# A tuned hybrid decoder block: two mixer forms rounded behind copies of products, three up weights' low parts behind the second token tile, gated tiles and a down sum ahead of low parts

## The chip, the cores and the metric

The kernel runs on one core of one Trainium2 chip. Its time is the device time of one execution, in microseconds (us). Three executions of the kernel before took 708.55, 709.43 and 709.46 us; the median is 709.43. A further execution was recorded by the hardware profiler; all rows of the profile and all durations are from that one.

## The reference, cut to what matters

One decoder layer on 512 tokens of 1024 channels, everything in float32:

```
h = rms_norm(x);  z = h @ w_in
y_pool = pool_mixer(z[pool]) @ w_pool_out
y_rnn  = rg_lru(z[rx]) * gelu(z[rg]) @ w_rg_out
x = x + rms_norm((sigmoid(z[gate_pool]) * y_pool + sigmoid(z[gate_rnn]) * y_rnn) @ w_o)
h = rms_norm(x);  up = h @ w_up                      # 1024 -> 2 x 3072
x = x + rms_norm((gelu(causal_conv(up[:3072])) * up[3072:]) @ w_down)
x = x + sigmoid(rms_norm(x) @ w_ple_gate) * rms_norm(p @ w_ple_proj)
```

## The kernel before

Engines are called by their short names: PE multiplies matrices, ACT (scalar engine) and DVE (vector engine) do the elementwise work, POOL (GpSimd) issues some transfers and takes the powers in the norms, SP issues the other transfers.

**Products.** A float32 product is made of three matmuls: every operand is split into a high part, which is the operand rounded to the type fp32r by a cast on ACT, and a low part, which the DVE makes by subtracting the high part from the operand. The helper `split` (L195 for the cast, L191 for the subtraction) and `prep` (L449, L191) do this; `mm3` (L222 to L224) issues high by high, high by low and low by high. Each split therefore costs one cast on ACT and one subtraction on DVE, and every matmul waits for them. The large products are moreover made in seven instead of eight block products (forms 1 to 7, in the order of `SEVEN`, `RSEVEN` and `SERIAL`). For these, sums and differences of blocks of the activations ("forms") are made on DVE and split, and sums of blocks of the weights lie in DRAM, made by transfers that POOL issues. Results of seven products are put together by copies and sums out of the PSUM banks (`ps`).

**Stages**, in the order of the PE: the input product with the mixers; the merge of the two mixers, which works on the products `rg` with w_rg_out (`rg_product`, two halves p, each with the forms 1, 5, 6, 2, 3, 7, 4); the w_o product in seven forms (`product("wo", ...)` with `o_form`); the first norm, per token tile of 128 tokens (four tiles); the product for the per-layer embedding (`ple_tile`, 12 matmuls of 512 columns for each tile); twelve pairs of tiles of the up product, the first one in plain blocks 11, 21, 12, 22 (`up_plain`, weights by `up_form(0, f)`), the others in seven forms (`up_product`); gating (`gated_half`, `hidden`); the down product in seven forms (`down_form`); and the per-layer gate. A token tile t goes through `x2_sum` and `x2_out`: two squares on ACT (L483), a sum s on DVE (L494), a power on POOL (L478), two `scalar_tensor_tensor` (L980) that make the residual, the same chain again for the next norm, and two more (L1053) that write the normalised halves `h2n`. `h2_tile` transposes each half on the PE (L991), splits it (cast L195 on ACT, low part L191 on DVE, both into tiles named `C`) and copies quarters of it to `h2f` on ACT (L1017).

**What sets the order.** The PE's order is the order of the code. The other engines' order is made ahead of time by a scheduler, which takes priorities: `urgent()` and `high_priority` put an instruction ahead of those recorded before it. Within an engine instructions run strictly in that order, so an instruction that waits holds up all behind it. `behind(ins, name)` adds an edge that orders `ins` after another instruction of the same engine. It adds no semaphore and no work.

**The names the change touches.** `last_copy` and `last_sub` hold the ACT cast and the DVE subtraction that `split` made last. `o_form(f)` (L878 to L891) makes form f of the merged activations for the w_o product and splits it into a quad `A`. Forms 1 and 2 are made within the second half of the merge, behind the products 6 and 7, the later ones within the w_o product. In `rg_product` a finished product f = 7 is copied twice by ACT, plain (L946) and negated (L947), to banks that the next products add onto. In the w_o product, L1067 copies the two banks of form 1 to the banks of form 2, and L1077 sums form 6 with form 5's copy into the banks of form 3. `up_form` makes the high and low part of a weight. In the gated stage, `hidden` (L1145) multiplies gate and up tiles into `h`; L1119 later writes negated products into the up banks that `hidden` reads. In the down product, L1350 subtracts product 7 from a kept copy `q5`, `down_form` makes and splits the forms, and L975 (`norm_of`) starts the next norm.

Edges that are in the kernel before and matter here: `up_form(1, f)` for f other than 1 has its cast behind `h2_done`, and for p above 2 form 6 has its cast behind `z_done`.

## Time and profile before

| what | value |
|---|---|
| three runs | 708.55, 709.43, 709.46 us, median 709.43 |
| the profiled execution | 708.84 us |
| its span | 707.1 us (1.74 us lie around it) |
| PE busy | 696.1 us, 98% of the span, 4423 instructions |
| PE weight loads (PEld) | 639.3 us, 90% (beside the matmuls) |
| DVE busy | 592.0 us, 84%, 772 instructions |
| ACT busy | 456.0 us, 64%, 693 instructions |
| POOL busy | 95.1 us, 13%, 123 instructions |
| mean granted clock of the PE | 0.996 |

How to read the views: a row of a timeline gives the start (us from the span's start), the duration, the engine, the line of the code, the operation, the tile written and the tiles read (buffer numbers left out), the size, how many instructions of this kind the row stands for, and, in brackets, the idle time ahead of the first of them and what ended it. A row of the view of waits gives who waited for whom, the total in us, how often and the longest. The view by windows gives busy microseconds of PE, PEld, DVE, ACT and POOL with their numbers of instructions, the granted clock of the PE, the share of the DMA engines, and GB/s. The busy time of the PE is near the whole span, so its few waits, and the stretches with a lower clock, are what is left beside the work itself.

### The profile page before, as it was taken

Reading aid. Unit: us, or ns where it says so; the run is one execution under the profiler, and the core shown is the slowest. Engines: PE = TensorE matmul, PEld = TensorE weight load, DVE = VectorE, ACT = ScalarE, POOL = GpSimd, SP = SyncE. Lnnn points to the kernel's source line nnn. Section 1 sums busy time; section 2 is a strip of 40 time slices with the busy share of each in tenths; the row PEclk is TensorE's granted clock in tenths of the full one; section 3 lists DMA queues with packets and bytes.
Section 4 is the critical chain, followed back from the end, with each engine's and each line's share of the span. In section 5 each row is a group of like instructions: output and inputs, shape, how many; then the busy total and the mean of one; then the engine's idle time right before and its main releaser. Section 6 shows DMA issues by size and latency. Waiting matters only on the chain.

```text
span 707.1 us, 11612 instructions
## 1 busy us (share of the span) xinstructions
PE 696.1 (98%) x4423; PEld 639.3 (90%) x4423; DVE 592.0 (84%) x772; ACT 456.0 (64%) x693; POOL 95.1 (13%) x123
## 2 busy tenths in 40 slices
PE   9999999999999999989999999999999999999997
PEld 7888888888889998879999999999999888888886
DVE  5698645999849898786989999999999998788972
ACT  5857789834547565478956776666667766665631
POOL 0321231421000000111013222221200000001100
PEclk9999999999999999999999999999999999999999
DMA  8999899999797897764379999999967576867111
GB/s 307 410 311 281 238 245 251 252 298 263 241 339 279 307 345 286 279 238 149 125 255 266 261 322 251 321 236 331 229 189 235 196 263 221 274 213 258 55 61 61
DMA packets 67288, 175.72 MB, mean 249 GB/s; under 512 B 6048, under 2 KB 6688, under 8 KB 66848
## 3 DMA queue, kind: packets, MB, share of 16 engines
q1 hardware_dynamic: 49808, 124.64, 49.9%
q0 software_dynamic: 17280, 50.34, 29.7%
q8 instruction: 35, 0.57, 0.3%
q14 instruction: 21, 0.17, 0.1%
q10 hardware_dynamic: 144, 0.00, 0.0%
HBM read 162.37 MB, written 62.91 MB: 319 GB/s over the span
## 4 chain that ended last, share of the span: by engine, by line
PE 84%; DVE 8%; ACT 3%; issue 2%; DMA 1%; POOL 1%; SPq 0%; ACTq 0%; DVEq 0%
PE ps L222 27%; PE ps L224 26%; PE ps L223 26%; PE ps L557 3%; DVE lo L191 2%; ACT rb L483 1%; PE ps L666 1%; DMA m<-in_x_t_dram 1%; DVE A L191 1%; POOL s L478 1%; DMA m<-in_rows_dram 1%; DVE m L1180 1%; DVE t L975 1%; DVE m L927 1%; ACT hi L195 1%
## 5 line engine op out<-in xcount | busy, mean ns | idle before, releaser
L191 DVE TENSOR_TENSOR lo<-raw,hi 128x1024 fp32r<-128x1024 f32 (+2 forms) x199 | 230.4, 1183 | 44.2 <-ACT hi L449 29.1
L222 PE MATMUL ps<-A,hi 128*128 128x256 f32 (+1 forms) x672 | 212.2, 316 | 0.8 <-ACT ps L1119 0.8
L223 PE MATMUL ps<-A,hi 128*128 128x256 f32 (+1 forms) x672 | 211.4, 315 | 0.0
L224 PE MATMUL ps<-A,lo 128*128 128x256 f32 (+1 forms) x672 | 211.4, 315 | 0.0
L449 ACT CAST hi<-raw 128x1024 fp32r<-128x1024 f32 (+1 forms) x118 | 118.3, 1013 | 57.0 <-PE ps L224 30.1
L222 PEld LDWEIGHTS ps<-A,hi 128*128 128x128 f32 x672 | 128.2, 191 | 9.3 <-issue 1.0
L224 PEld LDWEIGHTS ps<-A,lo 128*128 128x128 f32 x672 | 128.3, 191 | 6.9
L223 PEld LDWEIGHTS ps<-A,hi 128*128 128x128 f32 x672 | 128.2, 191 | 6.7
L222 PE MATMUL ps<-C,hi 128*128 128x256 f32 x376 | 103.7, 276 | 1.1 <-ACT ps L946 1.1
L224 PE MATMUL ps<-C,lo 128*128 128x256 f32 x376 | 103.2, 274 | 0.0
L223 PE MATMUL ps<-C,hi 128*128 128x256 f32 x376 | 103.2, 274 | 0.0
L195 ACT CAST hi<-raw 128x1024 fp32r<-128x1024 f32 x78 | 80.6, 1052 | 28.1 <-PE ps L223 18.3
L222 PE MATMUL ps<-hi,A 128*128 128x512 f32 x224 | 85.3, 381 | 0.6 <-ACT ps L1067 0.3
L223 PE MATMUL ps<-lo,A 128*128 128x512 f32 x224 | 84.9, 379 | 0.0
L224 PE MATMUL ps<-hi,A 128*128 128x512 f32 x224 | 84.9, 379 | 0.0
L222 PEld LDWEIGHTS ps<-C,hi 128*128 128x128 f32 x376 | 71.8, 191 | 1.8 <-ACT ps L946 1.3
L223 PEld LDWEIGHTS ps<-C,hi 128*128 128x128 f32 x376 | 71.8, 191 | 0.1
L224 PEld LDWEIGHTS ps<-C,lo 128*128 128x128 f32 x376 | 71.8, 191 | 0.0
L478 POOL TENSOR_TENSOR s<-s,mhalf 128x1 f32<-128x1 f32 (+1 forms) x21 | 15.2, 725 | 329.1 <-DVE s L494 306.4
L222 PEld LDWEIGHTS ps<-hi,A 128*128 128x128 f32 x224 | 42.3, 189 | 7.2 <-ACT ps L1067 0.7
L307 POOL DMA_DIRECT2D wdsum<-in_w_down_dram x36 | 33.3, 1087 | 110.2 <-ACT ps L1114 53.4
L224 PEld LDWEIGHTS ps<-hi,A 128*128 128x128 f32 x224 | 42.3, 189 | 6.0
(202 smaller groups left out, 1071.1 us busy)
## 6 DMA issues: line engine op xcount, KB each, us to landing
raw<-in_w_up_dram SPq DMA_DIRECT2D x46, 512.0 KB, 7.1
wdsum<-in_w_down_dram POOLq DMA_DIRECT2D x36, 512.0 KB, 9.7
raw<-in_w_in_dram SPq DMA_DIRECT2D x32, 512.0 KB, 7.8
raw<-wdsum SPq DMA_DIRECT2D x24, 512.0 KB, 4.3
raw<-in_w_down_dram SPq DMA_DIRECT2D x18, 512.0 KB, 4.2
wosum<-in_w_o_dram POOLq DMA_DIRECT2D x12, 512.0 KB, 8.7
wdsum<-wdsum POOLq DMA_DIRECT2D x12, 512.0 KB, 6.8
raw<-wosum SPq DMA_DIRECT2D x8, 512.0 KB, 6.7
```

Source lines behind the costliest of these rows:

```text
L191: return V.tensor_tensor(o, a, b, ALU.subtract)
L195: last_copy[0] = ACT.copy(hi, src)
L222: PE.matmul(o, ah, bh, start=start, stop=False, **kw)
L223: PE.matmul(o, ah, bl, start=False, stop=False, **kw)
L224: PE.matmul(o, al, bh, start=False, stop=stop, **kw)
L307: ins = nc.gpsimd.dma_start(o, i, **kw)
L449: ins = ACT.copy(hi, raw)
L478: last_pow[0] = nc.gpsimd.tensor_tensor(y, v, mhalf[:, :n], ALU.pow).ins.name
L483: ins = ACT.activation(rb, v, AF.Square, scale=1.0 / 32.0, accum_out=s)
L557: PE.matmul(rx[m], a[:, o : o + P], turns(b), start=k == 0 and i == 0, stop=k == KD - 1 and i == 2)
L666: PE.matmul(ps, bd[pr, a, o], turns(b[pr]), start=i == 0, stop=i == 2)
L927: V.tensor_tensor(g4, v.rearrange("p (h b a) -> p h a b", a=2, b=P), g4, ALU.mult)
```

## The change

All four parts add edges with `behind`; no instruction is added or removed on any engine.

1. In `o_form`, for the forms 2 and 5, the ACT cast is placed behind the instruction in `z_copied`: for form 2 the last negated copy of product f = 7 (L947), for form 5 the last copy L1067.
2. In `up_form(0, f)`, for f = 21, 12 and 22 the low part on DVE is placed behind the second half of `h2n` of token tile 1 (L1053), and for f = 12 and 22 the cast on ACT is placed behind the last ACT copy to `h2f` (L1017) that is recorded by then, of token tile 0.
3. In `up_form(1, 4)` the low part is placed behind the last gated tile `h` (L1145) that is recorded by then.
4. In `down_form(4, 2)` the low part is placed behind the first of the two sums L1350.

```diff
@@ -410,8 +410,14 @@
             t = b[p, {2: 21, 3: 22, 5: 0}[f]]
         hi, lo = (v.rearrange("p (j c) -> p j c", j=2) for v in parts_of(D))
         split(hi, lo, t)
+        if p == 0 and PLAIN.index(f) > 1:
+            behind(last_copy[0], h2f_done[0])
+        if p == 0 and PLAIN.index(f) > 0:
+            behind(last_sub[0], h2n_done[1])
         if p == 1 and f != 1:
             behind(last_copy[0], h2_done[0])
+        if (p, f) == (1, 4):
+            behind(last_sub[0], hid_done[0])
         if p > 2 and f == 6:
             behind(last_copy[0], z_done[0])
         ready["up", p, f] = (hi, lo)
@@ -812,6 +818,7 @@
 
 
     rp = {}
+    h2n_done, h2f_done, z_copied, hid_done, summed = {}, [None], [None], [None], {}
 
     def ple_tile(t):
         pair = []
@@ -887,6 +894,8 @@
             V.tensor_tensor(v, h11, h21, ALU.subtract)
         of[f] = quad("A").rearrange("p (s a) (b c) -> p s (a b) c", s=2, b=2)
         split(of[f][:, 0], of[f][:, 1], v)
+        if f in (2, 5):
+            behind(last_copy[0], z_copied[0])
 
     def o_lhs(f, k, i):
         v = of[f][:, :, k, i * P : (i + 1) * P]
@@ -944,7 +953,7 @@
                     ACT.activation(rb2[i][:, :HALF], z, AF.Identity, scale=-1.0)
                 elif f == 7:
                     ACT.copy(ra[i][:, HALF:], z)
-                    ACT.activation(rb2[i][:, HALF:], z, AF.Identity, scale=-1.0)
+                    z_copied[0] = ACT.activation(rb2[i][:, HALF:], z, AF.Identity, scale=-1.0).ins.name
             if p and f in (2, 3):
                 merge(p, int(f == 3), i, slice(0, HALF))
             elif f in (7, 4):
@@ -1014,7 +1023,8 @@
             if c == 0:
                 h2f[q] = {k: slot() for k in (0, 2)}
             for k in (0, 2):
-                ACT.copy(kept(h2f[q][k].rearrange("p (k c) -> p k c", k=2)[:, :, c * P : (c + 1) * P]), apart(ps[:, k : k + 2, :]))
+                v = kept(h2f[q][k].rearrange("p (k c) -> p k c", k=2)[:, :, c * P : (c + 1) * P])
+                h2f_done[0] = ACT.copy(v, apart(ps[:, k : k + 2, :])).ins.name
 
 
 
@@ -1050,7 +1060,8 @@
             r = rstd_of(res, after=after)
             for h in range(2):
                 h2n[t, h] = slot()
-                V.scalar_tensor_tensor(h2n[t, h], res[h], r, g_pre[h], ALU.mult, ALU.mult)
+                ins = V.scalar_tensor_tensor(h2n[t, h], res[h], r, g_pre[h], ALU.mult, ALU.mult)
+                h2n_done[t] = ins.ins.name
 
 
     o11, o12 = ra, rb2
@@ -1064,7 +1075,7 @@
                 o_form(SERIAL[n + 1])
             if f == 1:
                 with urgent():
-                    ACT.copy(o11[q - 2], oz[q - 2])
+                    z_copied[0] = ACT.copy(o11[q - 2], oz[q - 2]).ins.name
             if f == 7 and q == 2:
                 x2_norm(1, (o11[1], o12[1]))
             if last and q == 2:
@@ -1142,7 +1153,7 @@
                 ALU.add,
             )
             pu = hid[j]
-        V.tensor_tensor(hid[j], act_g[j], pu, ALU.mult)
+        hid_done[0] = V.tensor_tensor(hid[j], act_g[j], pu, ALU.mult).ins.name
 
     for t in range(NT):
         with tc.high_priority(offset=3 * URGENT):
@@ -1259,6 +1270,8 @@
             V.tensor_tensor(v, h11, h21, ALU.subtract)
         w = quad("A").rearrange("p (s a) (b c) -> p s (a b) c", s=2, b=2)
         split(w[:, 0], w[:, 1], v)
+        if (f, m) == (4, 2):
+            behind(last_sub[0], summed[0])
         down[f, m] = w
 
     def ahead_form(f, m):
@@ -1347,7 +1360,7 @@
         pass
     for i in range(2):
         with urgent():
-            V.tensor_tensor(q5[:, i], q5[:, i], zd[i], ALU.subtract)
+            summed[i] = V.tensor_tensor(q5[:, i], q5[:, i], zd[i], ALU.subtract).ins.name
     load_x3(1)
     x3_norm(0, (c11[0], c12[0]))
     x3_add(0)
```

In the changed kernel's file the lines stand 6 to 13 further down than in the one before (L946 is 955 there, L1067 is 1078, L1053 is 1063, L1017 is 1027, L975 is 984, L980 is 989, L826 is 833, L494 is 500, L1145 is 1156; L191 and L195 are the same).

What this does to the order on ACT at the merge and the first w_o product. `A` are the high parts of the forms (A441 is form 2, A472 form 5), `C427` the merged activations, `hi` the high parts of weights. Before:

```order
L946 COPY ps369_2057<-ps382_2131 128x256
L947 ACTIVATE ps377_2097<-ps382_2131 128x256
L195 CAST A441_2594<-C427_2479 128x1024
L946 COPY ps373_2077<-ps383_2132 128x256
L947 ACTIVATE ps381_2117<-ps383_2132 128x256
L449 CAST hi463_2663<-raw462_2661 128x1024
L449 CAST hi466_2688<-raw465_2686 128x1024
L1067 COPY ps369_2057<-ps457_2656 128x512
L449 CAST hi469_2701<-raw468_2699 128x1024
L195 CAST A472_2719<-C471_2717 128x1024
L1067 COPY ps373_2077<-ps458_2657 128x512
```

After:

```order
L955 COPY ps369_2057<-ps382_2131 128x256
L956 ACTIVATE ps377_2097<-ps382_2131 128x256
L955 COPY ps373_2077<-ps383_2132 128x256
L956 ACTIVATE ps381_2117<-ps383_2132 128x256
L195 CAST A441_2594<-C427_2479 128x1024
L455 CAST hi463_2663<-raw462_2661 128x1024
L455 CAST hi466_2688<-raw465_2686 128x1024
L1078 COPY ps369_2057<-ps457_2656 128x512
L455 CAST hi469_2701<-raw468_2699 128x1024
L1078 COPY ps373_2077<-ps458_2657 128x512
L195 CAST A472_2719<-C471_2717 128x1024
```

The two copies of the second product now stand ahead of form 2's cast, and the second L1067 copy ahead of form 5's.

On DVE at the second token tile, `lo538`, `lo554` and `lo558` are the low parts of the up weights 21, 12 and 22, m522 and m523 the normalised halves of token tile 1, s520 the sum of their norm, m453 and m454 the residual of token tile 2, m560 and m564 copies of embedding products, and C505 a low half of token tile 1. Before:

```order
L191 TENSOR_TENSOR lo538_3003<-raw536_3000,hi537_3002 128x1024
L191 TENSOR_TENSOR lo554_3036<-raw552_3033,hi553_3035 128x1024
L191 TENSOR_TENSOR lo558_3049<-raw556_3046,hi557_3048 128x1024
L494 SCALAR_TENSOR_TENSOR s520_2926<-s518_2922,s519_2924 128x1
L1053 SCALAR_TENSOR_TENSOR m522_2930<-m451_2644,s521_2928,m447_2635 128x512
L1053 SCALAR_TENSOR_TENSOR m523_2932<-m452_2646,s521_2928,m448_2636 128x512
L975 TENSOR_TENSOR t539_3012<-ps457_2656,m445_2631 128x512
L494 SCALAR_TENSOR_TENSOR s543_3020<-s541_3014,s542_3017 128x1
L826 COPY m560_3059<-ps555_3039 128x512
L826 COPY m564_3079<-ps562_3065 128x512
L980 SCALAR_TENSOR_TENSOR m453_2648<-t539_3012,s544_3022,m453_2648 128x512
L191 TENSOR_TENSOR C505_2882<-ps566_3085,C504_2881 128x4x128
```

After, from the first normalised half on (the sum s520 stands right ahead of it):

```order
L1063 SCALAR_TENSOR_TENSOR m522_2930<-m451_2644,s521_2928,m447_2635 128x512
L1063 SCALAR_TENSOR_TENSOR m523_2932<-m452_2646,s521_2928,m448_2636 128x512
L984 TENSOR_TENSOR t539_3012<-ps457_2656,m445_2631 128x512
L500 SCALAR_TENSOR_TENSOR s543_3020<-s541_3014,s542_3017 128x1
L833 COPY m560_3059<-ps555_3039 128x512
L989 SCALAR_TENSOR_TENSOR m453_2648<-t539_3012,s544_3022,m453_2648 128x512
L989 SCALAR_TENSOR_TENSOR m454_2650<-t540_3013,s544_3022,m454_2650 128x512
L984 TENSOR_TENSOR t575_3118<-sum461_2660,m446_2632 128x512
L833 COPY m564_3079<-ps562_3065 128x512
L191 TENSOR_TENSOR lo538_3003<-raw536_3000,hi537_3002 128x1024
L191 TENSOR_TENSOR lo554_3036<-raw552_3033,hi553_3035 128x1024
L191 TENSOR_TENSOR lo558_3049<-raw556_3046,hi557_3048 128x1024
```

The three low parts moved not only behind the two normalised halves but behind seven more instructions; the low half C505 of token tile 1 follows them now, as it did before. On ACT the casts of the weights 12 and 22 moved behind the four copies L1017 of token tile 0, and the squares of token tile 1's norm (L483) moved ahead of them. On SP three loads of sums of up weights (`raw<-up1sum`), which take the buffers of these three weights, are issued later, behind writes of results to DRAM.

On DVE at the first gated tiles, lo651 is the low part of up form (1, 4), lo654 and lo657 those of later weights, h647 and h648 the gated tiles. Before:

```order
L191 TENSOR_TENSOR lo651_3570<-raw649_3567,hi650_3569 128x1024
L1145 TENSOR_TENSOR h647_3563<-t637_3515,ps621_3303 128x512
L1145 TENSOR_TENSOR h648_3565<-t638_3521,ps622_3316 128x512
L191 TENSOR_TENSOR lo654_3602<-raw652_3599,hi653_3601 128x1024
L191 TENSOR_TENSOR lo657_3632<-raw655_3629,hi656_3631 128x1024
```

After:

```order
L1156 TENSOR_TENSOR h647_3563<-t637_3515,ps621_3303 128x512
L1156 TENSOR_TENSOR h648_3565<-t638_3521,ps622_3316 128x512
L191 TENSOR_TENSOR lo651_3570<-raw649_3567,hi650_3569 128x1024
L191 TENSOR_TENSOR lo654_3602<-raw652_3599,hi653_3601 128x1024
L191 TENSOR_TENSOR lo657_3632<-raw655_3629,hi656_3631 128x1024
```

The two gated tiles moved ahead of one low part; on ACT the two L1119 copies, which follow them, moved ahead of the fourth of four casts of weights. In the down product, the low part of form (4, 2) had stood ahead of the first sum L1350 and of a product `t` (L975); now `t` and the sum stand ahead of it, and the second `t` follows.

## The prediction

> **What bounds the kernel now.** I read the waits of the PE first, then the timelines of PE, ACT and DVE at each place where an edit falls, then the clock by windows. The view of waits lists, for each group, who was waited for, the us in total, how often, and the longest.
>
> ```profile
> PE ps L991 <- DVE m L1053: 1.6, 1, 1.6
> PE ps L222 <- ACT ps L946: 1.1, 1, 1.1
> PE ps L241 <- DVE mhalf L235: 1.1, 1, 1.1
> PE ps L222 <- ACT ps L1119: 0.8, 1, 0.8
> PE ps L991 <- DVE s L494: 0.5, 1, 0.5
> PE ps L557 <- ACT A L527: 0.5, 1, 0.5
> PE ps L222 <- ACT ps L1067: 0.3, 1, 0.3
> PE ps L222 <- DVE sum L1350: 0.3, 1, 0.3
> ```
>
> The PE is the bound, and it stands still only at single places of about a microsecond. The edits aim at six of these eight rows: L946 and L1067 (first edit), L1053 and L494 (second), L1119 (third), L1350 (fourth). Their sum, 4.6, is the most that the list itself promises. Two corrections follow. One is how a wait is counted: the list counts from the shown end of a matmul, but matmuls overlap.
>
> ```profile
> 258.90 0.28 PE L224 MATMUL ps<-A,lo 128*128 128x256 f32 x1
> 259.01 0.28 PE L222 MATMUL ps<-C,hi 128*128 128x256 f32 x1
> ```
>
> A 256-column matmul is shown 0.28 long, and the next starts 0.11 after it. A wait therefore costs about 0.17 more than listed. The other correction is larger: what is late next, once a wait is gone.
>
> **Place 1, merge and first w_o product (258 to 285).** ACT in before:
>
> ```profile
> 260.21 1.05 ACT L195 CAST A<-C 128x1024 fp32r<-128x1024 f32 x1 [1.70 <-DVE C L928]
> 261.17 0.37 ACT L946 COPY ps<-ps 128x256 f32<-128x256 f32 x1
> ```
> ```profile
> 268.42 1.05 ACT L195 CAST A<-C 128x1024 fp32r<-128x1024 f32 x1 [0.20 <-DVE C L878]
> 269.37 0.58 ACT L1067 COPY ps<-ps 128x512 f32<-128x512 f32 x1
> ```
>
> ACT stood idle 1.70 for the DVE's C, then rounded the form for 1.05, and only then copied a product that the PE had finished at 258.90 + 0.28 = 259.18. With the copy ahead it runs in that idle time. The listed 1.1 + 0.17 = 1.27 vanishes. So does the wait on the L1067 copy, which stood behind the cast of 268.42: 0.3 + 0.17 = 0.47. The PE is 1.74 earlier from 270 on. The first rounded form comes hardly later, since the copies fit into the 1.70 of idle time. The second now stands behind the L1067 copy of 0.58, about 0.5 later; queued behind it on ACT are only casts of weights. The next w_o products read the two forms, one of them 5 us away; I put the 0.5 at nothing, and at 0.5 without that cover. Next late is a sum on the DVE:
>
> ```profile
> 281.63 1.23 DVE L191 TENSOR_TENSOR A<-C,A 128x1024 fp32r<-128x1024 f32 x1 [0.21 <-ACT A L195]
> 282.77 0.69 DVE L1077 TENSOR_TENSOR ps<-sum,ps 128x512 f32<-128x512 f32 x1
> ```
> ```profile
> 284.35 0.38 PE L222 MATMUL ps<-hi,A 128*128 128x512 f32 x1
> ```
>
> L1077 ends at 283.46, and the PE adds onto its result at 284.35, 0.89 later. It stands behind a low part that waits for a cast of ACT, in a row of forms that no edit moves. The PE would come at 284.35 - 1.74 = 282.61, and find it ready only 283.46 plus some 0.06. So 0.91 of the 1.74 is given back: **-0.83**. Its ends are 0, if the row of forms slips as much again, and -1.74, if it moves with the PE. I take the middle, because the rows give it.
>
> **Place 2, second token tile (302 to 323).** DVE and ACT of before, and then three places of the PE:
>
> ```profile
> 302.63 3.49 DVE L191 TENSOR_TENSOR lo<-raw,hi 128x1024 fp32r<-128x1024 f32 x3
> 306.04 0.15 DVE L494 SCALAR_TENSOR_TENSOR s<-s,s 128x1 f32<-128x1 f32 x1
> 306.85 1.41 DVE L1053 SCALAR_TENSOR_TENSOR m<-m,s,m 128x512 f32<-128x512 f32 x2 [0.66 <-POOL s L478]
> 308.18 0.68 DVE L975 TENSOR_TENSOR t<-ps,m 128x512 f32<-128x512 f32 x1
> ```
> ```profile
> 301.89 1.05 ACT L195 CAST hi<-raw 128x1024 fp32r<-128x1024 f32 x1
> 302.84 0.64 ACT L483 ACTIVATE rb<-m 128x512 f32<-128x512 f32 x1
> ```
> ```profile
> 305.52 0.38 PE L223 MATMUL ps<-lo,m 128*128 128x512 f32 x1
> 305.73 0.38 PE L224 MATMUL ps<-hi,m 128*128 128x512 f32 x1
> 307.74 0.63 PE L991 MATMUL ps<-ident,m 128*128 128x128 f32 x4 [1.63 <-DVE m L1053]
> ```
> ```profile
> 316.27 0.27 PE L222 MATMUL ps<-C,hi 128*128 128x256 f32 x1
> ```
> ```profile
> 322.64 0.38 PE L222 MATMUL ps<-C,hi 128*128 128x256 f32 x1
> ```
>
> Three low parts of 3.49 stand ahead of the norm's sum s (L494). Behind them after the change, the sum waits only for its square, which takes the place of the cast at 301.89: about 301.9 + 0.64 + 0.1, so s at 302.7. With the same 0.81 from s to the halves (306.04 to 306.85), the halves are made from 303.5 to 304.9. The PE is free at 305.73 + 0.215 = 305.95 and finds them there: both stalls, 1.63 and 0.5, are gone. Eight transposes (0.63 for four, so about 1.0 for both halves) and the 24 matmuls before 316.27, at 0.215 each (305.52 to 305.73), put the first up matmul at about 312.0 instead of 316.27. This looks like 4.3, but the DVE pays. After the halves, from 304.9, come t and a copy (0.6 each), two L980 (1.3, released by POOL about then), another t and another copy: 3.8 in all. Only then, 308.7 to 312.1, come the three low parts; the low half of the second token tile, which the second up matmul reads, ends another 0.7 later, 312.8. The PE waits 0.8 there. Then a chain that the PE does not set:
>
> ```profile
> 318.21 1.41 DVE L980 SCALAR_TENSOR_TENSOR m<-t,s,m 128x512 f32<-128x512 f32 x2 [0.65 <-POOL s L478]
> ```
> ```profile
> 322.02 0.56 ACT L827 COPY m<-ps 128x512 f32<-128x512 f32 x1
> ```
>
> From the sum of the fourth tile, 0.8 ahead of 318.21, through L980 and four squares, to L827's copy, which ends at 322.58, 0.06 ahead of the matmul at 322.64 that takes its bank. This chain is why 322.64 was 322.64. After the change the low half at 312.8 releases ACT's copies of it (two sets of 0.6), a square of 0.64 on each side, and the sum comes at 316.1 rather than 317.4. Moving with it, the copy ends at 321.25. The PE's work from 316.27 to 322.64 holds 6.37, of which I take 6.2 to lie behind the second up matmul; it stands at its bank by 312.8 + 6.2 = 319.0, waits 2.3, and goes on at 321.30: **-1.34**. The ends: 0 where the chain is as late as before, and -4.3 where it follows the PE entirely. I take the chain's value since its durations are in the rows, and only its order differs. The three delayed low parts are read from about 315 on, when the first up product is through. The casts that the edit puts behind ACT's copies come before these low parts, and hold up only the next casts. SP's issues follow the buffers that these low parts free:
>
> ```profile
> 303.92 2.54 SPq L379 DMA_DIRECT2D raw<-up1sum  x3
> ```
>
> These three loads go out some 6 us later (low parts from 308.7 instead of 302.6), behind writes of results. They serve the second pair of up products, whose casts stand 30 us and more behind; I put them at nothing, and at up to 6 if they were wanted at once.
>
> The clock belongs to this place. Windows of before (the columns are busy us of PE, PEld, DVE, ACT, POOL, then the granted clock, DMA share and GB/s):
>
> ```profile
> 308.00:312.00 4.00, 3.45 (x14) 2.74 (x13) 4.00 (x9) 2.30 (x6) 0.54 (x1) 0.66 0.94 342
> 312.00:316.00 4.00, 4.00 (x18) 3.41 (x17) 3.23 (x6) 2.92 (x8) 0.54 (x1) 0.91 0.67 243
> ```
>
> The stalls of 1.63 and 0.5 were followed by a stretch at a lower clock, which lost 0.34 x 4 + 0.09 x 4 = 1.72 of full-speed time. It cost almost nothing in before, since the bank at 322.64 came no sooner. My new wait of 2.3 can bring it back, at a place with no cover. [...] I keep it as a rival below.
>
> **Place 3, first gated tiles (348 to 352).** DVE and ACT:
>
> ```profile
> 348.77 1.21 DVE L191 TENSOR_TENSOR lo<-raw,hi 128x1024 fp32r<-128x1024 f32 x1
> 349.90 1.27 DVE L1145 TENSOR_TENSOR h<-t,ps 128x512 f32<-128x512 f32 x2
> ```
> ```profile
> 347.43 3.91 ACT L195 CAST hi<-raw 128x1024 fp32r<-128x1024 f32 x4
> 351.23 0.65 ACT L1119 ACTIVATE ps<-ps 128x256 f32<-128x256 f32 x2
> ```
>
> L1119 writes the bank that L1145 reads. With L1145 ahead of the low part it ends 1.13 sooner, and in the new order the copies stand ahead of the fourth cast, at about 347.43 + 3 x 0.96 = 350.3, so that the first of them ends at 350.65. The PE, due 0.77 + 0.17 ahead of its present start, at 350.72, no longer waits: **-0.94**. The low part of form 4 is 1.3 later, and its product is one of the last of its pair, some 4.7 away: nothing. If the cast is nevertheless taken first, the gain is 0.
>
> **Place 4, down (641).** DVE:
>
> ```profile
> 639.67 1.22 DVE L191 TENSOR_TENSOR A<-h,A 128x1024 fp32r<-128x1024 f32 x1
> 640.80 0.68 DVE L1350 TENSOR_TENSOR sum<-sum,ps 128x512 f32<-128x512 f32 x1
> ```
>
> In the new order one t (L975) of 0.68 and the sum stand ahead of that low part: the sum ends at about 639.67 + 0.6 + 0.68 = 640.95 rather than 641.48, before the PE needs it. The stall of 0.3 with its 0.17: **-0.45**. The low part is read ten microseconds later. At worst the gain is 0.
>
> **The sum.** -0.83 - 1.34 - 0.94 - 0.45 = -3.56. The profiled run took 708.84, with 1.74 outside its span of 707.1: 705.3. It was 0.59 under the median of 709.43, so beside the runs shown I give 709.43 - 3.56 = **705.9**.
>
> **The rivals.**
> *Half clock after the new wait.* For it: the rows at 308 to 316. [...] Price 1.72, hardly covered: 707.6.
> *Place 2 yields nothing*, its chain being as late as before: 705.9 + 1.34 = 707.2. For it: DVE is full there, and every step that the low parts lose, they take again ahead of the low half.
> *Place 2 yields everything*, the chain following the PE: 705.9 - 3.0 = 702.9. Against it: four squares and L980 stand ahead of L827 in either order.
> *No effect*: the edits fix only an order, and engines in other rows of the trace absorb it: 709.4.
> [...]
>
> **How the numbers follow.** Forecast 0.52, own range 704.9 to 706.9; half clock 0.20; nothing at place 2 0.08; everything 0.06; no effect 0.07; slower 0.07. The range 704.0 to 708.2 holds the forecast, and the two rivals on the side of less gain, and lets the 0.9 of place 1 vanish. A measurement can tell about 0.2%, that is 1.4, from no change, so 708.0 divides faster from the same. Some of the half clock's 0.20 lies beyond: faster 0.83, same 0.10, slower 0.07.
>
> **What would show it.** Right: the waits on L946, L1067, L1053, L1119 and L1350 are absent after; a new wait on L1077 of about 0.9 near 283; a wait of about 0.8 on the low half near 312; one of about 2.3 on L827 near 320; the clock at 1.00 after it. Wrong: a granted clock under 0.9 near 321 to 325 (the half clock), a wait on one of the delayed low parts or casts, or PE's matmul at the bank still 1 us before the end of a copy that came at 322 (place 2 gave nothing).

## The result and the profile after

The changed kernel takes 708.17 us in the median of 22 runs (706.55 to 711.61), the kernel before 709.09 in 22 runs beside them. The ratio is 0.9988, with a 95% interval of 0.9976 to 0.9999. A second comparison, beside three of the experiments below, gave 709.64 against 709.04, ratio 1.0006 (0.9992 to 1.0020). The medians differ by 0.92 one way and 0.60 the other, and the two intervals together reach from 1.7 us faster to 1.4 slower: no gain shows in both. 705.9 was forecast. The profiled execution took 711.61 (span 709.8), the slowest of its 22, so it shows the harm larger than it is as a rule.

The waits of the PE in the changed kernel (who waited for whom, total, times, longest):

```profile
PE ps L222 <- ACT ps L1130: 2.8, 1, 2.8
PE ps L222 <- ACT m L834: 2.0, 1, 2.0
PE ps L222 <- issue: 1.1, 1, 1.1
PE ps L241 <- DVE mhalf L235: 1.1, 1, 1.1
PE ps L222 <- ACT ps L1125: 0.8, 1, 0.8
PE ps L223 <- DVE C L191: 0.8, 1, 0.8
PE ps L563 <- ACT hi L452: 0.5, 1, 0.5
```

The six waits that the edits aimed at are gone. Three of the new ones were forecast in kind and about in size: 2.0 on the bank copy (L834, formerly L827), 0.8 on the low half, and the 1.1 called "issue", which is the matmul that reads the sum L1088 (formerly L1077). The others were not: 2.8 on L1130, formerly L1119 but not at the place of the third edit, and 0.8 on L1125. The PE around three of these waits:

```profile
283.84 0.45 PE L222 MATMUL ps<-hi,A 128*128 128x512 f32 x1 [1.14 <-issue]
```
```profile
312.62 0.38 PE L223 MATMUL ps<-C,hi 128*128 128x256 f32 x1 [0.78 <-DVE C L191]
```
```profile
321.05 0.38 PE L222 MATMUL ps<-C,hi 128*128 128x256 f32 x1 [2.04 <-ACT m L834]
```

Follow single matmuls through both traces. Each row of this table is the start of the same matmul in the two timelines, and the difference says how far ahead the changed kernel is by then (at 214, ahead of every edit, it was 0.12 behind; in the other profiles of this document that start lies between 0.77 ahead and 1.20 behind, so that a lead in one profile is read against it).

| matmul | before | changed | difference |
|---|---|---|---|
| reader of the sum L1077 | 284.35 | 283.84 | -0.51 |
| taker of the bank of L827 | 322.64 | 321.05 | -1.59 |
| reader of L1119's bank, first gated tiles | 351.66 | 348.82 | -2.84 |
| the same one pair later (second bank) | 369.72 | 369.85 | +0.13 |
| the 23rd matmul after it | 372.28 | 374.11 | +1.83 |
| after the wait on L1125 | 495.68 | 498.86 | +3.18 |
| reader of the sum L1350 | 641.63 | 644.46 | +2.83 |

Up to 352 all went nearly as forecast, -2.84 with -3.11 for three places. Then one wait takes all of it back at once. ACT there, in the changed kernel and then in the kernel before:

```profile
363.70 0.37 ACT L1130 ACTIVATE ps<-ps 128x256 f32<-128x256 f32 x1
368.48 1.04 ACT L195 CAST hi<-raw 128x1024 fp32r<-128x1024 f32 x1 [4.41 <-DMA raw<-in_w_up_dram]
369.43 0.37 ACT L1130 ACTIVATE ps<-ps 128x256 f32<-128x256 f32 x1
```
```profile
367.36 1.05 ACT L195 CAST hi<-raw 128x1024 fp32r<-128x1024 f32 x1 [0.45 <-DMA raw<-in_w_up_dram]
368.32 0.36 ACT L1119 ACTIVATE ps<-ps 128x256 f32<-128x256 f32 x1
```

The second negated copy, for which the PE waits, stands behind the cast of a weight, and the cast waits for that weight's transfer. The PE and all elementwise work ahead are 3 us earlier than before, and the weight lands 1.1 later. Why it does, POOL shows, changed kernel first:

```profile
359.71 1.44 POOL L307 DMA_DIRECT2D wdsum<-in_w_down_dram  x2 [31.09 <-ACT ps L1125]
```
```profile
365.04 1.44 POOL L307 DMA_DIRECT2D wdsum<-in_w_down_dram  x2 [34.37 <-ACT ps L1114]
```

The first two transfers for the down sums are paced by an ACT copy (L1114, now L1125). They went out at 365.04, behind the weight's load (issued at 364.12). They go out at 359.71 now, 1.8 ahead of it (issued at 361.54), and the load takes 6.87 instead of 3.16. This load alone, with its time to landing, in before and in the changed kernel:

```profile
raw<-in_w_up_dram SPq DMA_DIRECT2D x1, 512.0 KB, 3.2
```
```profile
raw<-in_w_up_dram SPq DMA_DIRECT2D x1, 512.0 KB, 6.9
```

The copy came 5.3 earlier although the PE was only 2.9 ahead, because the order of the second gated tiles had changed. DVE of before, and of the changed kernel:

```profile
360.39 1.23 DVE L385 TENSOR_TENSOR sum<-raw,raw 128x1024 f32<-128x1024 f32 x1 [2.76 <-DMA raw<-in_w_up_dram]
361.53 1.40 DVE L1129 SCALAR_TENSOR_TENSOR t<-ps,col,t 128x510 f32<-128x510 f32 x2
```
```profile
354.91 1.53 DVE L1140 SCALAR_TENSOR_TENSOR t<-ps,col,t 128x511 f32<-128x511 f32 x2
358.45 1.23 DVE L385 TENSOR_TENSOR sum<-raw,raw 128x1024 f32<-128x1024 f32 x1 [2.01 <-DMA raw<-in_w_up_dram]
```

In before, the first tile's second conv step stood behind a sum of weight blocks that waited 2.76 for a load; the gelu waited for the step, and the second pacing copy stood behind the gelu and a cast. Now both conv steps of that tile stand ahead of the sum, and the copies come soon after. No edit names these instructions. The order of a kernel with the third edit alone shows the same turn; with the first alone, with the second alone, and with the first, second and fourth together it is that of before.

Behind the wait the clock falls. The columns are the stretch and its length, the busy us of PE, PEld, DVE, ACT and POOL, then the granted clock, the DMA share and GB/s:

```profile
366.00:370.00 4.00, 1.17 (x11) 0.97 (x10) 2.38 (x4) 1.52 (x4) 0.00 (x0) 1.00 0.39 145
370.00:374.00 4.00, 4.00 (x23) 4.00 (x24) 2.28 (x3) 2.33 (x6) 1.32 (x2) 0.60 0.57 186
```

The granted clock is 0.60 over 4 us (half clock, 0.50, from 370.76 to 374.18), and 1.70 more is lost by 374.11 (from +0.13 to +1.83). The further 1.35 before 499 has a like form: a cast (491.31) waited for a load that was issued at 473.20 and took 18.1 (14.4 in before), and the work that leads to the second L1125 copy, on which the PE waited, is queued behind it. No experiment was made on that one; a second profile of the changed kernel, further below, does not have it.

### The profile page after: what moved, and what is told of

Read it like the earlier page. It is cut to its first block, busy times and chain, and to the rows that moved or that the text cites. A ratio compares the mean times of both kernels' runs of the same rounds, so it can differ in the third digit from the quotient of the medians.

```text
span 709.8 us, 11608 instructions
## 1 busy us (share of the span) xinstructions
PE 695.8 (98%) x4423; PEld 639.9 (90%) x4423; DVE 592.3 (83%) x772; ACT 454.7 (64%) x693; POOL 94.7 (13%) x123
## 4 chain that ended last, share of the span: by engine, by line
PE 70%; DVE 12%; DMA 8%; ACT 6%; issue 3%; POOL 0%; SPq 0%; DVEq 0%; ACTq 0%
PE ps L222 22%; PE ps L224 22%; PE ps L223 22%; DMA raw<-in_w_up_dram 4%; PE ps L563 3%; DVE lo L191 3%; ACT m L166 1%; DVE m L701 1%; DMA parts<-hi 1%; ACT t L166 1%; DVE m L628 1%; ACT hi L195 1%; DVE t L772 1%; PE ps L672 1%; DMA raw<-in_w_pool_out_dram 1%
## 5 line engine op out<-in xcount | busy, mean ns | idle before, releaser
L191 DVE TENSOR_TENSOR lo<-raw,hi 128x1024 fp32r<-128x1024 f32 (+2 forms) x199 | 230.9, 1187 | 51.1 <-ACT hi L455 30.3
L195 ACT CAST hi<-raw 128x1024 fp32r<-128x1024 f32 x78 | 80.4, 1051 | 33.2 <-PE ps L223 16.2
```

The lines of the kernel that those rows point to most:

```text
L191: return V.tensor_tensor(o, a, b, ALU.subtract)
L195: last_copy[0] = ACT.copy(hi, src)
```

## The experiments

**Theory (collision):** the third edit turns the order of the second gated tiles; this lets the first down sums out ahead of a weight's load; the load lands late, and the copy behind its cast holds the PE. **Rivals:** the stage from 352 on is held by its transfers in any order and absorbs every gain (bandwidth); or the loss is the half clock behind the new wait near 320 (clock).

### The third edit taken back

```diff
-        if (p, f) == (1, 4):
-            behind(last_sub[0], hid_done[0])
```

> The changed kernel without its third edit (the low part of up form (1, 4) stands where it stood before). Collision theory: the third edit alone turns the order of the second gated tiles on DVE and ACT, which lets the first two down sums of POOL go out 5 us earlier, into the load of an up weight; without it POOL's sums go out near 362 to 365, that load takes some 3.2 to 4 us instead of 6.87, the wait of 2.8 at 369 is absent, and the gains of places 1, 2 and 4 are kept: 2.6 under the kernel before, ratio 0.9963 (0.995 to 0.9975). The wait of 0.8 on the copy at 351 is back. Rival, bandwidth: the stage from 352 on is held by its loads wherever the PE stands, so an earlier PE waits there in any order: ratio 0.9988 as for the whole change. Rival, clock: the loss is a half-clock stretch after the new wait of 2.0 near 320, which this kernel has as well: ratio 0.9988.

Measured: 706.40 against 708.97, ratio 0.9971 (0.9958 to 0.9985): faster than before by 2.57 in the medians (2.1 by the ratio), where the whole change was 0.92 faster or 0.60 slower. In the profile the sums go out at 361.88, behind the load (issued 360.95, landed in 3.61), and the wait of 2.8 is absent; the one at the place of the edit is back, with 0.6. The gain expected was 2.6.

### The third edit alone

```diff
+        if (p, f) == (1, 4):
+            behind(last_sub[0], hid_done[0])
```

(to the kernel before, without the other three)

> The kernel before with the third edit alone. Collision theory: at 351 the PE gains 0.9 as forecast, but the second gated tiles turn round, POOL's first two sums go out near 361 to 362, the load of the up weight issued near 363 takes 6 to 7 us, and the copy behind its cast comes some 3 us late; the PE waits 2 to 3 near 369, at times with a half-clock stretch of 1.7 after it. Sum: 1 to 3.5 slower than before, ratio 1.0015 to 1.005. Rival, that the edit gains what it removes and other edits do the harm: 0.9987. Rival bandwidth (the stage absorbs any gain): 1.000.

Measured: 710.85 against 708.99, ratio 1.0022 (1.0011 to 1.0034): slower, by little but clear of no change. An edit that takes away a wait of 0.94 costs 1.9 in the medians (0.8 to 2.4 by the interval). ACT and POOL of it:

```profile
370.18 1.04 ACT L195 CAST hi<-raw 128x1024 fp32r<-128x1024 f32 x1 [3.18 <-DMA raw<-in_w_up_dram]
371.13 0.37 ACT L1124 ACTIVATE ps<-ps 128x256 f32<-128x256 f32 x1
```
```profile
363.03 1.44 POOL L307 DMA_DIRECT2D wdsum<-in_w_down_dram  x2 [31.12 <-ACT ps L1119]
```

The same sequence as in the changed kernel: sums early, a load of 5.63, the cast held 3.18 by it. The rivals stated for it predicted no loss. This one profile does not show the whole 1.9: its PE was 1.20 late at 214, ahead of the edit; at the place of the edit it gains 0.93, and by 372 it has lost 1.63 again, behind a wait of 1.2 and with no half clock. Most of the rest goes with the half clock, as told further below: nine of the twelve runs had a stretch of it (median 711.66), three had none (709.49).

### The first sums left for the next form

```diff
-            if f in SUMS_AFTER and p >= SUMS_FROM:
+            if f in SUMS_AFTER and (p > SUMS_FROM or (p == SUMS_FROM and f != 1)):
```

> The changed kernel, but the two down sums that POOL issues after form 1 of pair 2 are left out there, so that the sums begin after form 6 of that pair; all sums are still made, each two a step later. Collision theory: the load of the up weight issued near 361 takes 3.2 to 4 us instead of 6.87, the cast behind it runs before 366, the wait of 2.8 at 369 is absent: ratio 0.995 (0.994 to 0.9965). It could lose some of that where the last sums come later. Rivals bandwidth and clock: 0.9988.

Measured: 706.38 against 708.97, ratio 0.9955 (0.9940 to 0.9970), in six runs from 705.39 to 707.07. POOL and ACT, and loads of the same stretch (355 to 367) in this kernel and in the changed one, with their median time to landing:

```profile
367.48 1.45 POOL L307 DMA_DIRECT2D wdsum<-in_w_down_dram  x2 [39.40 <-ACT ps L1130]
```
```profile
365.31 1.05 ACT L195 CAST hi<-raw 128x1024 fp32r<-128x1024 f32 x1 [0.95 <-DMA raw<-in_w_up_dram]
366.27 0.37 ACT L1130 ACTIVATE ps<-ps 128x256 f32<-128x256 f32 x1
```
```profile
raw<-in_w_up_dram SPq DMA_DIRECT2D x3, 512.0 KB, 3.4
```
```profile
raw<-in_w_up_dram SPq DMA_DIRECT2D x3, 512.0 KB, 6.9
```

The order of the gated tiles is the changed one here; only the sums' place differs. So it is their traffic, not the order by itself. The load behind the sums took 6.87 in the changed kernel, 2.0 times the 3.40 of this one, and in the four other profiles in which the sums went out first it took 5.63 to 6.17, or 1.7 to 1.8 times. This profile also has the half clock of the first rival of the prediction, right behind the wait of 2.0 near 320:

```profile
320.00:324.00 4.00, 3.50 (x17) 3.51 (x18) 3.35 (x9) 3.66 (x10) 0.54 (x1) 0.60 0.94 350
```

Between 320.5 and 324.2 the PE loses 1.63 of its 2.14 lead, and the execution still took only 706.38.

### The late cast behind the copy

```diff
+        if (p, f) == (2, 3):
+            behind(last_copy[0], paced[0])
```

> The changed kernel, and the cast of the up weight that lands late is placed behind the second negated copy of form 6 of pair 2 on ACT, so that the copy no longer stands behind a cast that waits for a transfer. The transfers are as in the changed kernel. Collision theory, in its part that the harm reaches the PE only through this copy: the load still takes 6 to 7 us, but the wait of 2.8 at 369 is absent: ratio 0.995 (0.994 to 0.9965). Rival bandwidth: the weight itself or the next one is late for the PE, and the wait appears 1 to 3 us further on: 0.9988. Rival clock: 0.9988.

Measured: 706.59 against 708.97, ratio 0.9955 (0.9938 to 0.9972). ACT:

```profile
364.35 0.37 ACT L1132 ACTIVATE ps<-ps 128x256 f32<-128x256 f32 x1 [1.07 <-DVE h L1151]
366.82 1.05 ACT L195 CAST hi<-raw 128x1024 fp32r<-128x1024 f32 x1 [2.10 <-DMA raw<-in_w_up_dram]
```

The sums go out early (358.76) and the load is as late as ever (6.07), but the copy no longer stands behind the cast, and no wait appears further on. So the weight itself was not wanted yet; only the order on ACT carried its lateness to the PE.

### The second gated tiles back in the old order

```diff
-            add(b[p, 0], b[p, 11], b[p, 12])
+            ins = V.tensor_tensor(b[p, 0], b[p, 11], b[p, 12], ALU.add)
+            if p == 3:
+                behind(conv[2, 2], ins.ins.name)
...
-        if (p, f) == (1, 4):
+        if (p, f) in ((1, 4), (3, 1)):
...
+                    if (p, i) == (2, 0):
+                        behind(gelu[2], paced[0])
```

> The changed kernel with all four edits, and edges that put the second gated tiles back into the order of before (second conv step behind the first sum of weight blocks on DVE, the gelu behind the first copy on ACT, one low part behind the gated tiles). Collision theory: POOL's first sums go out 5 us later than in the changed kernel, no wait of 2.8 at 369, all four gains kept: 3.5 under the kernel before, ratio 0.995 (0.994 to 0.9965). Rivals bandwidth and clock: 0.9988.

Measured: 707.32 against 708.97, ratio 0.9981 (0.9964 to 0.9998). In the profile (an execution of 705.80) the sums go out at 362.52, behind the load (361.60, landed in 3.40), and the wait at 369 is absent. The size is under what was expected, and the upper end of its interval reaches nearly to 1: the runs go from 705.80 to 711.79, and the profile is of the shortest. The order did what the theory says, but the time does not confirm its size. Part of what is missing stands in the profile: the old order has a wait of its own once the PE is this early.

```profile
361.74 0.38 PE L222 MATMUL ps<-A,hi 128*128 128x256 f32 x1 [0.82 <-ACT ps L1127]
```

The L1127 copy stands behind the late gelu again, and the PE's lead falls from 3.57 to 2.51 there. What held the longest runs is open.

### Without the sums' traffic

The kernel before and the changed one, both without POOL's transfers for the down sums, the down product reading plain blocks in their place, so that they do not compute the reference's result:

```diff
+        if name == "wd":
+            return block_of(name, f % 4, q)
...
-            if f in SUMS_AFTER and p >= SUMS_FROM:
+            if 0:
```

> The kernel before without the transfers of POOL that make the down sums; the down product reads plain blocks of w_down in their place, so its result is not the reference's. It is the base for the next kernel. Collision theory: it was little held by this traffic: 706 to 708.5, ratio 0.997 to 1.000, a narrow spread, and its waits are those of before. Rival bandwidth: it is held by the traffic from 352 to 540, and gains several us, ratio under 0.995.

> The changed kernel without the same transfers, and with the same reading of plain blocks. Collision theory: the load of the up weight near 361 takes 3.2 to 3.5 us, there is no wait at 369, and the kernel is 3.0 to 3.6 under the same kernel before without the sums (ratio of the two medians 0.995 to 0.996), about 1.6 less where the clock falls after the wait near 320. Rival bandwidth or gate order by itself: the two differ by about 0.9, as with the sums (0.9988).

Measured: 709.04 for the kernel before without the sums, ratio 1.0006 (0.9992 to 1.0019): it had not been held by them. The changed one without them took 706.29, ratio 0.9957 (0.9940 to 0.9974), 2.75 under the other (ratio of the medians 0.9961). In its profile the load took 3.60, and there is no wait at 369. With the traffic the changed kernel was 0.92 faster than before or 0.60 slower, without it 2.75 faster; the distance is the collision's price. The profiled execution (706.43) had the half-clock stretch near 320 again. The bandwidth rival falls: it wanted 0.9 here, and several us from the kernel before without sums.

### The first edit alone, and the second alone

To the kernel before, without the other three, first

```diff
+        if f in (2, 5):
+            behind(last_copy[0], z_copied[0])
```

> The kernel before with the first edit alone. By the rows at 283 (the sum L1077 is next late): 0.5 to 0.8 at 284; but the chain of token tiles at 302 to 322 hangs on the DVE and ACT, and passes on only what they gain themselves: 0.4 to 0.8 in all, ratio 0.9990 to 0.9995. Rival, that the whole 1.74 is kept: 0.9976. Rival, that place 2 absorbs everything: 1.000.

Measured: 707.83 against 708.99, ratio 0.9984 (0.9975 to 0.9993): 1.16, a little over the 0.4 to 0.8 expected; in the trace the lead is 0.81 at the reader of the sum, 0.76 at the bank copy and 1.01 at 641, of which 0.17 was there at 214. The last 0.35 of it came at 641 itself, at the sum L1350, though the fourth edit is not in this kernel.

and then

```diff
+        if p == 0 and PLAIN.index(f) > 1:
+            behind(last_copy[0], h2f_done[0])
+        if p == 0 and PLAIN.index(f) > 0:
+            behind(last_sub[0], h2n_done[1])
```

> The kernel before with the second edit alone. By the chain at place 2: 1.2 to 1.3 under the kernel before, ratio 0.9982; a wait of 0.8 on the low half and one of 1 to 2 on the L827 copy near 320, and the order at the second gated tiles as before. Rival bandwidth: the gain is lost behind 352, ratio 1.000. Rival clock: the wait near 320 costs a half-clock stretch in most executions and takes the gain away, 1.000 or over.

Measured: 708.28 against 708.99, ratio 0.9986 (0.9970 to 1.0002), 0.7 of the 1.3 expected, and not clear of no change. The waits of 2.0 and 0.8 are in its profile; the PE is 1.11 further ahead at the bank copy than at 214. By 640 it has lost 1.0 of this again, most of it around a wait of 0.45 near 559, in the down product, that no other profile here has.

### The changed kernel again

No edit; it ran beside the kernels without sums and the last version.

> The changed kernel once more, beside the next three. Collision theory: again a wait on the L1130 copy near 369, of a length that differs from one execution to the next with the landing of one load (0.5 to 3), and so the widest spread of times: 706.5 to 711, ratio 0.9988. Rival, that the long wait belonged to one unlucky execution: no such wait in this profile, and a ratio near 0.995.

Measured: the 709.64 told at the top. Its profile, of an execution of 708.29:

```profile
PE ps L222 <- ACT m L834: 2.0, 1, 2.0
PE ps L222 <- ACT ps L1130: 1.3, 1, 1.3
```

The wait on L1130 is there again, shorter, and the half clock came near 321 instead of 371 (granted clock 0.57 from 321 to 325). So the wait is no accident of one execution, but its length varies. The spread, 708.29 to 713.56, is hardly wider than that of the kernel before beside it (707.99 to 712.90), against expectation.

### Place 2 in another order

On DVE, both low halves of token tile 1 first, one low part behind them, and the other two behind the residual of the fourth tile; with the cast behind the copy (shown for place 2 alone, against the changed kernel).

```diff
-            behind(last_sub[0], h2n_done[1])
+            low0[f] = last_sub[0]
...
             h2_tile(1)
+            behind(low0[21], last_low[0])
             x2_out(2, h2_done[0])
             x2_sum(3, (oz[1], o5[:, 1]))
+            for f in (12, 22):
+                behind(low0[f], added[0])
```

> The changed kernel with the cast behind the copy at 366 (as in the experiment with that cast), and at place 2 another order on DVE: both low halves of token tile 1 first, then one of the three low parts, and the other two behind the residual of the fourth tile. By the chain at place 2: the wait of 0.8 on the low half vanishes, the sum of the fourth tile comes near 313.9 instead of 315.8, the copy that frees the bank ends near 319.0 instead of 321.0, and the wait there is about 0.9 instead of 2.0: 1.9 less than with the cast alone, ratio to before 0.993 (0.991 to 0.9945), and no half-clock stretch near 320. Rival: the two delayed low parts are late for their products near 319 to 321, or the chain is held elsewhere: 0.9955 as with the cast alone.

Measured: 705.70 against 708.99, ratio 0.9961 (0.9942 to 0.9979); not clearly better than the cast alone. The first half of the expectation came true: the wait of 0.8 on the low half is gone, and the PE takes the bank 1.5 earlier than with the cast alone. Then it stood for another copy:

```profile
321.53 0.38 PE L222 MATMUL ps<-C,hi 128*128 128x256 f32 x1 [1.36 <-DVE m L836]
```
```profile
317.81 1.22 DVE L191 TENSOR_TENSOR lo<-raw,hi 128x1024 fp32r<-128x1024 f32 x1
319.46 1.41 DVE L1069 SCALAR_TENSOR_TENSOR m<-m,s,m 128x512 f32<-128x512 f32 x2 [0.44 <-POOL s L486]
320.79 1.28 DVE L836 COPY m<-ps 128x512 f32<-128x512 f32 x2
```

DVE has only 0.44 us of idle time in these rows, and the low parts pushed out of one chain had gone ahead of the copies that free the next bank.

### A version from the findings

The first sums left for the next form, the late cast behind the copy, and at place 2 the third low part behind these DVE copies (shown for the third low part alone, against the version above):

```diff
-            for f in (12, 22):
-                behind(low0[f], added[0])
+            behind(low0[12], added[0])
...
+    behind(low0[22], low0["copy"])
     for kind, n in O_AFTER:
```

> A version made from the findings: the changed kernel, with the first two down sums left for the next form, with the late cast behind the copy at 366, and at place 2 the two low halves first, one low part behind them, the second behind the residual of the fourth tile, and the third behind the DVE copies that free the banks near 320. By the rows of the low-half experiment, its new wait of 1.4 on a DVE copy near 321 goes away, and the wait on the ACT copy near 318 stays at 0.8: about 703.5, ratio 0.9925 (0.991 to 0.9945). Rival: the third low part or the low part for the next pair is late now, and the time stays near 705.5, ratio 0.9955.

Measured: 704.95 against 709.04, ratio 0.9950 (0.9934 to 0.9966), the fastest median, though its interval overlaps those of the two single repairs. It is 1.4 short of the 703.5 expected: the wait on L836 is gone and the 0.8 on the ACT copy stays, as expected, but a low half of the last token tile, near 328, is late now:

```profile
PE ps L222 <- ACT m L837: 0.8, 1, 0.8
PE ps L223 <- DVE C L191: 0.6, 1, 0.6
```

## Why the prediction was wrong

*Place 1, -0.83 forecast:* -0.63 in the table (-0.51, with 0.12 behind at 214). The mechanism was right. The sum itself came 0.28 later than before, since the forms' chain slipped a little.

*Place 2, -1.34 forecast:* -1.08. Both new waits came, 0.8 and 2.0 for 0.8 and 2.3. The whole 4.3, which the PE seemed to be promised, was not to be had, as argued.

*Place 3, -0.94 forecast:* -0.93 at the spot itself (from -1.91 to -2.84, by the trace).

*Place 4, -0.45 forecast:* -0.45 (from +3.28 to +2.83). Whether the fourth edit did it is not shown. The profiles with the first, the second or the third edit alone, which lack the fourth, gain 0.35 at the same matmul and have no wait there; only the kernel before, with its sums and without, has it. No run has the fourth edit alone.

Together with 0.2 from a small wait near 344 this is about -3.3, for -3.56. In the profile of the late cast behind the copy, which has neither the wait at 369 nor a half clock near 320, the PE gains 3.51 from 214 to 641. So the sum of the local terms was right. Even the signs that the prediction named were right: the waits went, the new ones came, and the clock was 1.00 from 321 to 325 in the first profile. All these signs lie at the places of the edits.

*What failed is the sum*, and in it the sentence of place 3 that costs the delayed low part at "nothing" and lets the gain of 0.94 stand. I looked for who reads the moved instruction. I did not look at what the order does behind it, on the same engines, at the next pair, where nothing had been edited; there it turned, and with it the copy that paces POOL's first transfers. The net of the third edit is +1.9 (710.85 against 708.99), not -0.94. The collision takes 1.7 to 3.2 from the whole change (0.92 faster or 0.60 slower with it, 2.59 faster with the sums later). That the first median, 708.17, lies just inside the range of 704.0 to 708.2 does not speak for the forecast; the second, 709.64, lies outside.

*The second thing that was wrong is the chance of the half clock,* 0.20, an estimate of the author's. With the collision removed the medians are 2.4 to 2.75 under before (by the ratios 0.9955 and 0.9957 it is 3.0 to 3.2, with intervals that hold 3.56). The half clock behind the wait of 2.0 was granted in the profiles of three kernels (sums later, no sums changed, changed again), and not in those of five others with the same wait. It cost 1.63 in the one followed above, where 1.72 was forecast. For the other runs the mean granted clock of each is on record. In the fourteen profiles a mean of 0.996 to 0.998 goes with a stretch of half clock of 3.41 us within the work, and 0.999 or 1.000 with none. Read so, the three kernels without the collision that keep all four edits in the changed order (sums later, late cast behind the copy, no sums changed) had a stretch in 10 of their 21 runs. The 11 others have medians of 705.49, 705.58 and 705.31, or 3.4 to 3.7 under before, where 3.56 was forecast; the 10 have 706.38, 706.83 and 707.00. In the kernel before, runs with a stretch are no slower (708.95 against 708.97 beside the first experiments), as the prediction had argued from the cover there. These groups are small, and where the stretch lies is known only for the profiled runs.

What the profiles show ahead of it: in before the clock falls at 309.28, for 3.41 us, and again at the end of the span, at 705.22; in the changed kernel it falls at 370.76, for 3.41 us, and at 708.68. The two falls lie 116 times 3.413 us apart in before and 99 times in the changed kernel, both within 0.04. So I count windows of 3.41 us from a profile's own falls. The window ahead of the stretch with the sums later, and the emptiest one near 320 in the profile of the changed kernel, which has the same wait of 2.0 there and no stretch behind it:

```profile
317.35:320.76 3.41, 1.37 (x13) 1.13 (x12) 2.75 (x6) 3.26 (x10) 0.54 (x1) 1.00 0.71 226
```
```profile
319.60:323.01 3.41, 1.96 (x17) 1.97 (x18) 2.68 (x5) 3.38 (x11) 0.62 (x2) 1.00 0.70 257
```

In the first (sums later) nearly the whole wait lies in one window, and the PE is busy for 40% of it; in the second it is cut in two, and the PE is busy for 57%. In the window ahead of the stretch in before (from 305.86) the PE is busy for 36%, and ahead of the one at 370.76 in the changed kernel for 27%. These are few profiles, and what makes the clock fall is not shown beyond them.

*Slower* stood at 0.07. The one kernel that is clearly slower, the third edit alone, lacks the second edit and has no wait of 0.8 on the low half; its wait of 1.6 on the bank copy stands in the profile of the first edit alone as well, which is faster than before. *That place 2 yields nothing or everything* did not come true.

## What to carry to other kernels

When an order edge makes a stage earlier, compare the order on every engine beyond the place of the edit as well, up to the next points where something paces transfers: an elementwise instruction that releases a bulk transfer is a trigger, and here 5.3 us on it decided whether a load ran behind the sums' transfers (6.87) or ahead of them (3.16). The late load did harm here only through the copy behind its first reader: with the copy ahead of the cast the load was as late (6.07), and the wait of 2.8 was gone. So the copy that the PE waits for belongs ahead of a cast that waits for a transfer. Measure each of several edits alone: here the first gained, the second probably did, and the third took most of it back; the fourth was not run alone. And look for signs of being wrong behind the places of the edits as well, since all those at the places came out as forecast.

## What the runs showed of the hardware

The load of 512 KB near 361 took 3.16 to 3.6 us where the first two sums' transfers went out behind it or not at all, and 5.6 to 6.9 where they went out 1.3 to 2.0 us ahead of it. A wait of the PE of 2.0 us was followed by a stretch of 3.41 us at half clock in three profiles, and not in five others. In the one of the three that is followed above, the PE was busy for 40% of the 3.41 us ahead of the stretch; in the changed kernel, one of the five, for 57% of the emptiest window near that wait.
